# A hybrid decoder step: sample attention as one step generator, state update first in a chunk, values' split queued later

## The chip, the cores and the metric

One core of a Trainium2 chip. The metric is the device time of one launch in microseconds (us). The kernel is one program on the core's five engines: TensorE (PE in the profile) multiplies into PSUM, VectorE (DVE), ScalarE (ACT) and GpSimd (POOL) work element by element, SyncE (SP) issues nearly all DMAs. Each engine takes its instructions in the order in which they were written for it; they wait for one another by semaphores.

## What is computed

One step of a single decoder layer with two groups of heads. 512 prompt tokens and 8 x 8 sample tokens are normalised and projected together (576 columns); the result feeds sparse attention (8 heads, with an indexer that keeps 256 keys) and gated linear attention (GLA, 4 heads); both are gated and projected out.

```python
def dsa_sample(qa, ka, va, qi, ki, wi, cache_k, cache_v, cache_idx_k, page_table):
    ...
    sc = jnp.where(causal[None], index_scores(qi, wi, ki_all), -jnp.inf)
    _, idx = lax.top_k(sc, topk)
    ...
    return sparse_attend(qa, k_sel, v_sel, valid)

def gla(q, k, v, log_a, s0):
    def step(S, inp):
        ...
        o = o_inter + jnp.einsum('bhts,bhsv->bhtv', att, vt)
        S_new = jnp.exp(last)[:, :, 0, :, None] * S + jnp.einsum('bhsk,bhsv->bhkv', kt * jnp.exp(last - cum), vt)
        return S_new, o
```

The sample tokens' keys and values lie in pages of 128 tokens in device memory, found by a page table: 8 sequences of 8 pages.

## The kernel before, in words

All projections run in fp32 split into a high part and a remainder: a weight piece `w_raw` (256 KB) is loaded by SyncE (L178), cast to `w_hi` on ScalarE (L181), and the remainder `w_lo` is taken on VectorE (L183); three matmuls stand for one. `wload` holds this, `gemm` a projection of 128 outputs (ps_g, L219), `vgroup` one of 512 value columns, with the tokens as rows (L604 to L610).

**The sample units.** Sample attention is four `unit`s: two halves of the heads (`hg`) times two groups of four sequences (`w`). A unit reads its K pages in two halves of 16 pages (tile `kt`, four pages of 256 KB in a tile; matmuls `pS`), adds the new tokens, takes the softmax (`pr`, exponential at L780), transposes the probabilities (`pt`, L787, copied to `prT`), and reads its V pages in two halves (tile `vt`, matmuls `pOs`). I call the units 1 to 4 in their order, and a half of K or V a group; there are 16 groups. A unit is a Python generator with a `yield` behind each part; `fill()` (behind each half `gemm` and each second piece of `vgroup`) runs it on by a rate of 0.42 or 0.40 steps a fill. So the rate spreads the units between the projections. Tiles `kt` and `vt` share a pool of five buffers (units 1, 2) or four (3, 4). The page requests (`page_dma`) are written where the tile is used, and ordered on SyncE by `issue_after(paged[-3])`.

**The values.** `vgroup` copies its four token tiles out of PSUM as `v_tok` on ScalarE (L637), from where SyncE stores them to `sv` in device memory (L639); the samples' values go as `v_smp`. The tiles have tag `e1`, two buffers.

**GLA.** For each of four heads: `log_decay` (`ps_z`, from the loaded gate weights `wg`), `exps` (decay tiles `lv_d`, multiplied by k and q on VectorE, L994, L995), `decays` (transposed keys `kDt`, intra-chunk products `pl`), then `recur`. That one loads the head's values (`vtok`, and `vSg` for the samples), splits `vSg` into `vs` (four casts on ScalarE, L1069), and runs four chunks: output `pO`, state update `pUg`, copy `osb`, squares `jk` for the norm (L1086). Then come the samples: states `st` loaded for even and odd sequences, products into one `pO`, and updates `pUg` by `Kb` and `vs`. `ps_z`, `pO`, `pUg`, `pt`, `pl` and `ps_v` share three PSUM buffers (`pm`).

The heads' GLA is woven into the projections, so units 3 and 4, the value groups 2 and 3 and the GLA heads 0 to 3 run between 640 and 960 us. The order on each engine follows from the order of the text, from `high_priority(offset=WOFF)` (weights, and the matmuls of a `run` behind its first), from `issue_after`, and from when buffers come free; a scheduler settles it at build time.

```python
        with tc.issue_after(wloads[-1]):
            sy.dma_start(vtok, sv[:TP].rearrange("(i p) c -> p i c", p=P))
            sy.dma_start(vS[:TS], sv[TP:])
...
            with tc.issue_after(mark):
                for r0 in (0, 32):
                    se.copy(vs[w][r0 : r0 + 32], vS[r])
```

`mark` is the copy of `kDt` (L967).

Of the kernel before, what the change touches and what calls it, by code (L numbers as in the profile page):

```python
# [10 lines left out]
F32 = mybir.dt.float32  # L11
# [9 lines left out]
P = 128  # L21
# [98 lines left out]
def build(tc, I, O):  # L120
# [4 lines left out]
    R0, R1, RF = 0.42, 0.4, 1.1  # L125
# [21 lines left out]
    paged, wloads = [], []  # L147
# [447 lines left out]
    def vgroup(g, step):  # L595
# [39 lines left out]
        for i in range(4):  # L635
            vt = ev.tile([P, 512], F32, name="v_tok", tag="e1", bufs=2)
# [104 lines left out]
    def unit(un, w, hg, pages):  # L741
        span = 4
        qz = ev.tile([P, 4, 4, 32], F32, name="qz", tag="e0", bufs=2)
        po_.memset(qz, 0.0)
        for g in range(4):
            src = qaS[:, 4 * hg + g, 32 * w : 32 * w + 32].rearrange("p (b t) -> p b t", t=DT)
            dst = qz[:, g].rearrange("p b t -> p (b t)")
            dst = bass.AP(tensor=dst.tensor, offset=dst.offset, ap=[dst.ap[0], [40, 4], [1, DT]])
            po_.tensor_copy(dst, src)
        pr = un.tile([P, PAST + TS], F32, name="pr")  # L750
        mx = un.tile([P, 8], F32, name="mxs", bufs=2)
        lsel = [selw[:, 256 * half + P * w : 256 * half + P * (w + 1)] for half in range(2)]
        for half in range(2):
            S = pm.tile([P, 512], F32, name="pS", tag="pu", bufs=1)
            pe.matmul(S, lsel[half], biasS[:, :512], start=True, stop=False)
            for b0 in range(0, 4, span):
                mms = []
                for bb in range(b0, b0 + span):
                    kt = un.tile([P, 4, 512], F32, name="kt", tag="kv", bufs=pages)
                    page_dma(lambda j: kt[:, j, :], lambda r: I["ck"][r, hg].rearrange("o d c -> (o d) c"), (4 * w + bb) * NPAGE + 4 * half, 4)  # L760
                    kv = kt.rearrange("p j (g s) -> p j g s", g=4)
                    mms[:0] = [
                        partial(pe.matmul, S[32 * g : 32 * g + 32], qz[:, g, bb, :], kv[:, :, g, :], start=False, stop=(bb == 4 - span), tile_position=(0, 32 * g))
                        for g in range(4)
                    ]
                run(*mms)
                yield
            se.copy(pr[:, 512 * half : 512 * half + 512], S)
            ve.reduce_max(out=mx[:, half : half + 1], in_=pr[:, 512 * half : 512 * half + 512], axis=AX.X)
        S = pm.tile([P, 512], F32, name="pS", tag="pu", bufs=1)  # L770
        pe.matmul(S[:, :TS], lsel[1], biasS[:, 512:], start=True, stop=False)
        run(*(
            partial(pe.matmul, S[32 * g : 32 * g + 32, :TS], qaS[:, 4 * hg + g, 32 * w : 32 * w + 32], kaS[:, 4 * hg + g, :], start=False, stop=True, tile_position=(0, 32 * g))
            for g in range(4)
        ))
        se.copy(pr[:, PAST:], S[:, :TS])
        ve.reduce_max(out=mx[:, 2:3], in_=pr[:, PAST:], axis=AX.X)
        ve.reduce_max(out=mx[:, 3:4], in_=mx[:, 0:3], axis=AX.X)
        ve.tensor_scalar(out=mx[:, 3:4], in0=mx[:, 3:4], scalar1=-SCALE, scalar2=None, op0=ALU.mult)
        se.activation(pr, pr, AF.Exp, bias=mx[:, 3:4], scale=SCALE, accum_out=mx[:, 4:5])  # L780
        ve.reciprocal(out=mx[:, 7:8], in_=mx[:, 4:5])
        prT = un.tile([P, 9, P], F32, name="prT")
        for c in range(3):
            pt = mm1("pt")
            if c < 2:
                for j in range(4):
                    pe.transpose(pt[:, P * j : P * (j + 1)], pr[:, 512 * c + P * j : 512 * c + P * (j + 1)], ident)  # L787
                se.copy(prT[:, 4 * c : 4 * c + 4, :], pt.rearrange("p (j r) -> p j r", j=4))
            else:
                pe.transpose(pt[:, :P], pr[:, PAST + TS - P :], ident)  # L790
                se.copy(prT[:, 8, :], pt[:, :P])
        yield
        pO = pm.tile([P, 512], F32, name="pOs", tag="pu", bufs=1)
        for j0 in range(0, NPAGE, span):
            mms = []
            for j in range(j0, j0 + span):
                vt = un.tile([P, 4, 512], F32, name="vt", tag="kv", bufs=pages)
                page_dma(
                    lambda bb: vt[:, bb, :], lambda r: I["cv"][r, :, 512 * hg : 512 * hg + 512].rearrange("o s c -> (o s) c"),
                    NB * NPAGE + 4 * (NPAGE * w + j), 4,  # L800
                )
                mms[:0] = [
                    partial(
                        pe.matmul, pO[32 * g : 32 * g + 32].rearrange("p (b d) -> p b d", b=4), prT[:, j, 32 * g : 32 * g + 32],
                        vt[:, :, P * g : P * (g + 1)], start=(j == span - 1), stop=False, tile_position=(0, 32 * g),
                    )
                    for g in range(4)
                ]
            if j0 == NPAGE - span:
                mms += [  # L810
                    partial(
                        pe.matmul, pO[32 * g : 32 * g + 32].rearrange("p (b d) -> p b d", b=4), prT[:, 8, 32 * g : 32 * g + 32],
                        vaS[:, P * h : P * (h + 1)].unsqueeze(1).to_broadcast([P, 4, P]), start=False, stop=True, tile_position=(0, 32 * g),
                    )
                    for g in range(4) for h in (4 * hg + g,)
                ]
            run(*mms)
            yield
        ob = pr[:, :512]
        se.activation(ob, pO, AF.Copy, scale=mx[:, 7:8])  # L820
        pt = mm1("pt")
        for bb in range(4):
            pe.transpose(pt[:, P * bb : P * (bb + 1)], ob[:, P * bb : P * (bb + 1)], ident)
        src = bass.AP(tensor=pt.tensor, offset=pt.offset, ap=[pt.ap[0], [32, 4], [P + DT, 4], [1, DT]])
        sl = (slice(None), slice(4 * hg, 4 * hg + 4), slice(32 * w, 32 * w + 32))
        ve.tensor_tensor(
            out=mixS[sl].rearrange("p g (b t) -> p g b t", t=DT), in0=src,
            in1=gaS[sl].rearrange("p g (b t) -> p g b t", t=DT), op=ALU.mult,
        )
        yield  # L830
# [19 lines left out]
    us = chain(unit(un, 0, 0, 5), unit(un, 1, 0, 5))  # L850
    filler[:] = [us, R0, 0.0]
# [10 lines left out]
    us = chain(unit(un, 0, 1, 4), unit(un, 1, 1, 4))  # L862
    filler[:] = [us, R1, 0.0]
# [90 lines left out]
    def decays(h, qT, kT, cum, eL, kD, wide):  # L954
# [7 lines left out]
        def rows_of_k():  # L962
# [4 lines left out]
            mark = se.copy(kDt, pt.rearrange("p (i d) -> p i d", i=4))  # L967
# [5 lines left out]
            kept[h] = eL, qE, kDt, ks, getattr(mark, "ins", mark)  # L973
# [84 lines left out]
    def recur(h, eL, qE, kDt, ks, mark):  # L1058
# [17 lines left out]
        for i in range(4):  # L1076
            tsl = slice(P * i, P * (i + 1))
            pO = mm1("pO")
            pe.matmul(pO[:, :DV], att[:, i, :], vtok[:, i, :], start=True, stop=(S is None))
            pU = mm1("pUg")  # L1080
            pe.matmul(pU[:, :DV], kDt[:, i, :], vtok[:, i, :], start=True, stop=True)
# [4 lines left out]
            se.activation(jk, pO[:, :DV], AF.Square, accum_out=ss[:, i : i + 1])  # L1086
# [9 lines left out]
        pe.matmul(pO[:, :DV], attS, vS, start=True, stop=False)  # L1096
        for e in range(2):
            st = gl.tile([P, 4, DV], F32, name="st", bufs=2)
            sview = lambda x: x[h].rearrange("p (m e) v -> p m e v", e=2)[:, :, e, :]
            sy.dma_start(st, sview(I["state"]))  # L1100
            for m in range(4):
                mp_ = slice(32 * m, 32 * m + 32)
                pe.matmul(pO[mp_, :DV], Qb[:, 2 * m + e, :], st[:, m, :], start=False, stop=(e == 1), tile_position=(0, 32 * m))
# [254 lines left out]
```

## Time and profile before

| | |
|---|---|
| median of 3 runs | 1238.5 us (1237.82 to 1240.36) |
| profiled execution | 1241.06 us, its span 1239.3 us |
| TensorE busy | 1216.5 us (98%) |
| VectorE, ScalarE, GpSimd busy | 662.8, 564.6, 301.8 us |
| mean granted clock of TensorE | 0.995 |
| moved | 209.42 MB, 169 GB/s over the span |

The profile's page gives busy times, a strip of 40 slices, the DMA queues, the chain of waits and the costliest groups of instructions. An engine's idle time matters only where TensorE, the busiest, waits for it. The granted clock is given in parts of 2.4 GHz; a mean between 0.5 and 1 over a stretch means that a part of it ran at 1.2 GHz.

### The profile page before, as it was taken

What the parts mean: (1) busy time and instruction counts of PE and PEld (TensorE: products, weight loads), DVE (VectorE), ACT (ScalarE), POOL (GpSimd) and SP (SyncE); (2) the same over time, 40 slices, a digit from 0 to 9 for tenths busy, and PEclk for the clock granted to TensorE, in tenths of its full rate; (3) what the DMA queues carried; (4) which work ended last, traced back from release to release, by engine and by line L of the source; (5) the groups of instructions that cost most, each with busy time, mean ns of one, the idle gap of its engine ahead of it and who ended that gap; (6) DMA issues with size and microseconds to landing.
All of it is one profiled execution on the core that took longest, in us unless ns stands there. A gap on an engine that the chain in (4) does not pass through costs nothing.

```text
span 1239.3 us, 23602 instructions
## 1 busy us (share of the span) xinstructions
PE 1216.5 (98%) x8699; PEld 1073.9 (87%) x8699; DVE 662.8 (53%) x1326; ACT 564.6 (46%) x1079; POOL 301.8 (24%) x471
## 2 busy tenths in 40 slices
PE   9999999999999999999999989999999999999996
PEld 8899987899997878898987778678999998888896
DVE  6679899699744314434545244425566463223233
ACT  7967655453443323443444253435566462223233
POOL 1224567445411201010105210301124020202021
PEclk9999999999999999999999999999999999999999
DMA  9642233423457596753667573765525364333335
GB/s 315 219 151 91 65 108 101 158 86 104 162 176 243 181 314 207 254 190 139 218 206 248 188 261 111 267 214 199 168 75 186 106 204 145 107 96 121 94 107 174
DMA packets 126885, 209.42 MB, mean 169 GB/s; under 512 B 14497, under 2 KB 37554, under 8 KB 126066
## 3 DMA queue, kind: packets, MB, share of 16 engines
q1 hardware_dynamic: 125682, 206.47, 50.7%
q8 instruction: 68, 1.11, 0.4%
q10 hardware_dynamic: 1088, 1.45, 0.4%
q14 instruction: 47, 0.39, 0.1%
HBM read 184.52 MB, written 23.22 MB: 168 GB/s over the span
## 4 chain that ended last, share of the span: by engine, by line
PE 86%; DVE 5%; DMA 4%; ACT 2%; issue 1%; SPq 1%; POOL 0%; ACTq 0%; DVEq 0%; POOLq 0%
PE ps_g L219 36%; PE ps_g L227 6%; PE acc L1224 5%; PE acc L1223 5%; PE acc L1222 5%; PE ps_g L608 4%; PE ps_g L610 4%; PE ps_g L609 4%; PE pOs L255 2%; PE pS L255 2%; PE acc L1227 1%; PE acc L1226 1%; DMA vSg<-sv 1%; PE ps_v L604 1%; PE ps_v L605 1%
## 5 line engine op out<-in xcount | busy, mean ns | idle before, releaser
L181 ACT CAST w_hi<-w_raw 128x512 fp32r<-128x512 f32 x316 | 193.4, 619 | 371.7 <-PE ps_g L219 135.0
L183 DVE TENSOR_TENSOR w_lo<-w_raw,w_hi 128x512 fp32r<-128x512 f32 x252 | 177.8, 712 | 308.2 <-ACT w_hi L181 286.8
L219 PE MATMUL ps_g<-xh,w_hi 128*128 128x288 f32 x1312 | 289.0, 299 | 1.4 <-issue 1.0
L219 PE MATMUL ps_g<-xl,w_hi 128*128 128x288 f32 x1312 | 287.9, 298 | 0.0
L219 PE MATMUL ps_g<-xh,w_lo 128*128 128x288 f32 x1312 | 286.4, 297 | 0.0
L219 PEld LDWEIGHTS ps_g<-xh,w_hi 128*128 128x128 f32 x1312 | 213.6, 189 | 10.0 <-issue 5.8
L219 PEld LDWEIGHTS ps_g<-xl,w_hi 128*128 128x128 f32 x1312 | 213.1, 189 | 2.0 <-issue 1.2
L219 PEld LDWEIGHTS ps_g<-xh,w_lo 128*128 128x128 f32 x1312 | 213.4, 189 | 1.2 <-DVE w_lo L199 0.2
L1223 PE MATMUL acc<-w_lo,mh 128*128 128x512 f32 (+1 forms) x320 | 110.7, 346 | 0.0
L1224 PE MATMUL acc<-w_hi,ml 128*128 128x512 f32 (+1 forms) x320 | 110.7, 346 | 0.0
L1222 PE MATMUL acc<-w_hi,mh 128*128 128x512 f32 (+1 forms) x320 | 110.3, 346 | 0.0
L608 PE MATMUL ps_g<-w_hi,xh 128*128 128x512 f32 x256 | 101.5, 398 | 0.0
L610 PE MATMUL ps_g<-w_hi,xl 128*128 128x512 f32 x256 | 100.1, 391 | 0.0
L609 PE MATMUL ps_g<-w_lo,xh 128*128 128x512 f32 x256 | 99.8, 390 | 0.0
L183 POOL TENSOR_TENSOR w_lo<-w_raw,w_hi 128x512 fp32r<-128x512 f32 x64 | 86.4, 1353 | 51.8 <-ACT w_hi L181 38.7
L1242 POOL TENSOR_TENSOR y<-y,nfb 128x512 f32<-128x512 f32 (+3 forms) x25 | 27.7, 1121 | 186.8 <-ACT yjk L1241 186.8
L1223 PEld LDWEIGHTS acc<-w_lo,mh 128*128 128x128 f32 x320 | 60.5, 189 | 7.5
L1222 PEld LDWEIGHTS acc<-w_hi,mh 128*128 128x128 f32 x320 | 60.4, 189 | 7.5
L1224 PEld LDWEIGHTS acc<-w_hi,ml 128*128 128x128 f32 x320 | 60.4, 189 | 7.5
L608 PEld LDWEIGHTS ps_g<-w_hi,xh 128*128 128x128 f32 x256 | 48.0, 188 | 13.1 <-issue 2.5
L610 PEld LDWEIGHTS ps_g<-w_hi,xl 128*128 128x128 f32 x256 | 48.1, 188 | 11.2 <-issue 0.8
L609 PEld LDWEIGHTS ps_g<-w_lo,xh 128*128 128x128 f32 x256 | 48.1, 188 | 9.5
(339 smaller groups left out, 1952.8 us busy)
## 6 DMA issues: line engine op xcount, KB each, us to landing
w_raw<-in_w SPq DMA_DIRECT2D x188, 256.0 KB, 3.0
kt<-in_ck SPq DMA_DIRECT2D x128, 256.0 KB, 5.1
vt<-in_cv SPq DMA_DIRECT2D x128, 256.0 KB, 5.4
w_raw<-in_wv SPq DMA_DIRECT2D x64, 256.0 KB, 3.0
w_raw<-in_wo SPq DMA_DIRECT2D x64, 256.0 KB, 2.7
xr<-in_xT SPq DMA_DIRECT2D x16, 288.0 KB, 4.6
xt<-in_xp SPq DMA_DIRECT2D x4, 1024.0 KB, 7.5
sv<-v_tok SPq DMA_DIRECT2D x16, 256.0 KB, 3.3
```

What stands on the lines that cost most here:

```text
L181: se.copy(hi, raw)
L183: lo_eng[0].tensor_tensor(out=lo, in0=raw, in1=hi.bitcast(F32), op=ALU.subtract)
L219: pe.matmul(ps[:, j, :HT], wt, xt[:, j * HT : (j + 1) * HT], start=(k == 0 and n == 0), stop=(k == NK - 1 and n == 2),)
L227: pe.matmul(ps[:, 0, :TQ], wt[:, c], xt[:, P:T], start=(k == 0 and n == 0), stop=(k == NK - 1 and n == 2))
L255: f()
L608: pe.matmul(accs[i], xh[k][:, c], wh, start=a, stop=False)
L609: pe.matmul(accs[i], xh[k][:, c], wl, start=False, stop=False)
L610: pe.matmul(accs[i], xl[k][:, c], wh, start=False, stop=b)
L1222: pe.matmul(acc, mh[k][:, tsl], wh, start=(k == 0), stop=False)
L1223: pe.matmul(acc, mh[k][:, tsl], wl, start=False, stop=False)
L1224: pe.matmul(acc, ml[k][:, tsl], wh, start=False, stop=(k == NK - 1))
L1242: po_.tensor_tensor(out=yc, in0=yc, in1=nfb[:r, cs], op=ALU.mult)
```

## The change

Five parts, all in the order and the buffers; the arithmetic stays.

- `unit` becomes one generator `units` for both units of a half of the heads. It takes exactly one step a fill (rate 1.0): `rest(n)` pads it with empty steps. `fetch` asks for the next group's 16 pages right behind the step that used the group before.
- `v_tok` takes turns between tags `e1` and `e0`, two buffers each (`e0` is also that of `qz`, `oT` and others).
- In `recur`, `vSg` is loaded ahead of `vtok`, and the casts `vs` are issued behind the last `w_hi` cast written so far (`rounded[-1]`), not behind the copy of `kDt`.
- In a chunk the state update `pUg` goes ahead of the output `pO`; `jk` squares `osb` (SBUF), not `pO` (PSUM).
- Both state tiles are loaded first; the eight products with `st` come in one run, then the updates.

```diff
-    R0, R1, RF = 0.42, 0.4, 1.1
+    RF = 1.1
...
-            se.copy(hi, raw)
+            c = se.copy(hi, raw)
+            rounded.append(getattr(c, "ins", c))
...
-            vt = ev.tile([P, 512], F32, name="v_tok", tag="e1", bufs=2)
+            vt = ev.tile([P, 512], F32, name="v_tok", tag=("e1", "e0")[i % 2], bufs=2)
...
-    def unit(un, w, hg, pages):
+    def units(un, hg, pages):
+        def fetch(w, part, half):
+            out = []
+            for n in range(4 * half, 4 * half + 4):
+                t = un.tile([P, 4, 512], F32, name=("kt", "vt")[part], tag="kv", bufs=pages)
+                if part:
+                    page_dma(
...
+                out.append(t)
+            return out
+        def rest(n):
+            for _ in range(n):
+                yield
+        kv = fetch(0, 0, 0)
+        yield
+        for w in range(2):
...
+            for half in range(2):
...
+                run(*mms)
+                yield
+                kv = fetch(w, half, 1 - half)
+                se.copy(pr[:, 512 * half : 512 * half + 512], S)
+                ve.reduce_max(out=mx[:, half : half + 1], in_=pr[:, 512 * half : 512 * half + 512], axis=AX.X)
+                if not half:
+                    yield from rest(3)
...
+            se.activation(pr, pr, AF.Exp, bias=mx[:, 3:4], scale=SCALE, accum_out=mx[:, 4:5])
+            ve.reciprocal(out=mx[:, 7:8], in_=mx[:, 4:5])
+            yield
...
+            yield from rest(2)
+            pO = pm.tile([P, 512], F32, name="pOs", tag="pu", bufs=1)
+            for half in range(2):
...
+                run(*mms)
+                yield
+                if not half:
+                    kv = fetch(w, 1, 1)
+                    yield from rest(3)
+                elif w == 0:
+                    kv = fetch(1, 0, 0)
...
+            yield from rest(2)
...
-    us = chain(unit(un, 0, 1, 4), unit(un, 1, 1, 4))
-    filler[:] = [us, R1, 0.0]
+    us = units(un, 1, 4)
+    filler[:] = [us, 1.0, 0.0]
...
         with tc.issue_after(wloads[-1]):
+            sy.dma_start(vS[:TS], sv[TP:])
             sy.dma_start(vtok, sv[:TP].rearrange("(i p) c -> p i c", p=P))
-            sy.dma_start(vS[:TS], sv[TP:])
...
-            with tc.issue_after(mark):
+            with tc.issue_after(rounded[-1]):
...
+            pU = mm1("pUg")
+            pe.matmul(pU[:, :DV], kDt[:, i, :], vtok[:, i, :], start=True, stop=True)
             pO = mm1("pO")
             pe.matmul(pO[:, :DV], att[:, i, :], vtok[:, i, :], start=True, stop=(S is None))
-            pU = mm1("pUg")
-            pe.matmul(pU[:, :DV], kDt[:, i, :], vtok[:, i, :], start=True, stop=True)
...
-            se.activation(jk, pO[:, :DV], AF.Square, accum_out=ss[:, i : i + 1])
+            se.activation(jk, osb[:, i, :], AF.Square, accum_out=ss[:, i : i + 1])
...
+        sts = [gl.tile([P, 4, DV], F32, name="st", bufs=2) for _ in range(2)]
         for e in range(2):
-            st = gl.tile([P, 4, DV], F32, name="st", bufs=2)
-            sy.dma_start(st, sview(I["state"]))
-            for m in range(4):
-                pe.matmul(pO[mp_, :DV], Qb[:, 2 * m + e, :], st[:, m, :], start=False, stop=(e == 1), tile_position=(0, 32 * m))
+            sy.dma_start(sts[e], sview(I["state"], e))
+        run(*(
+            partial(pe.matmul, pO[32 * m : 32 * m + 32, :DV], Qb[:, 2 * m + e, :], sts[e][:, m, :], start=False, stop=(e == 0), tile_position=(0, 32 * m))
+            for e in (1, 0) for m in range(4)
+        ))
```

Three places show how the instructions move. Line numbers behind the change are some 27 higher in this part of the program (L1069 becomes L1096, L780 becomes L806).

SyncE between value group 2 and the values' load of head 0, before. `w_raw` are weight pieces, `kt` pages of K for unit 4, `sv` the stores of the values; `TENSOR_LOAD` and `ISA` read page numbers.

```order
L178 DMA w_raw<-in_w 128x512 x2
L639 DMA sv_475<-v_tok 128x512 x3
L178 DMA w_raw<-in_w 128x512
L639 DMA sv_475<-v_tok 128x512
L178 DMA w_raw<-in_w 128x512
L152 TENSOR_LOAD ptab
```

The same place of SyncE with the change:

```order
L178 DMA w_raw<-in_w 128x512 x2
L640 DMA sv_475<-v_tok 128x512 x4
L152 TENSOR_LOAD ptab
L157 ISA
L157 DMA kt<-in_ck 128x512
L157 ISA
L157 DMA kt<-in_ck 128x512
L178 DMA w_raw<-in_w 128x512 x2
L1090 DMA vtok<-sv_475 128x4x256
```

The four stores stand together, and two K pages stand ahead of the two weight pieces that stood between and behind the stores. Further on, `vSg` still follows `vtok`, two pages, the store of `v_smp` and eight more pages.

ScalarE at the softmax of unit 4 and the split of head 1's sample values (`vs`), before.

```order
L181 CAST w_hi<-w_raw 128x512 x3
L1069 CAST vs_10335<-vSg 32x256 x2
L181 CAST w_hi<-w_raw 128x512
L1069 CAST vs_10336<-vSg 32x256 x2
L776 COPY pr<-pS 128x64
L780 ACTIVATE pr,mxs<-pr,mxs 128x1088
L637 ACTIVATE v_tok<-ps_g,sst 128x512 x2
```

The same place of ScalarE with the change:

```order
L802 COPY pr<-pS 128x64
L806 ACTIVATE pr,mxs<-pr,mxs 128x1088
L181 CAST w_hi<-w_raw 128x512 x2
L815 COPY prT<-pt 128x512 x2
L638 ACTIVATE v_tok<-ps_g,sst 128x512 x2
L818 COPY prT<-pt 128x128
L638 ACTIVATE v_tok<-ps_g,sst 128x512 x2
L181 CAST w_hi<-w_raw 128x512
L1096 CAST vs_10391<-vSg 32x256 x2
L1096 CAST vs_10392<-vSg 32x256 x2
```

The score copy and the exponential stood behind the four casts `vs`; now the casts stand behind them, and behind the copies of the transposed probabilities and the four `v_tok`.

TensorE at the first chunks of head 0, before; `ps_g` is a projection that fills the gaps.

```order
L219 MATMUL ps_g<-xl,w_hi 128x288 x2
L1079 MATMUL pO<-vtok,att 128x256
L1081 MATMUL pUg<-vtok,kDt 128x256
L1079 MATMUL pO<-vtok,att 128x256
L219 MATMUL ps_g<-xh,w_hi 128x288 x2
```

The same place of TensorE with the change:

```order
L220 MATMUL ps_g<-xl,w_hi 128x288 x2
L1106 MATMUL pUg<-vtok,kDt 128x256
L1108 MATMUL pO<-vtok,att 128x256
L1106 MATMUL pUg<-vtok,kDt 128x256
L220 MATMUL ps_g<-xh,w_hi 128x288 x2
```

The three PSUM buffers go to an output, an update and an output before, and to an update, an output and an update now; the output of the second chunk comes after the gap.

## Rows read from the trace of the kernel before

**Rows 1.** The page: span, and TensorE in part 1 (busy us, share, instructions).
```profile
span 1239.3 us, 23602 instructions
...
PE 1216.5 (98%) x8699; PEld 1073.9 (87%) x8699; DVE 662.8 (53%) x1326; ACT 564.6 (46%) x1079; POOL 301.8 (24%) x471
```

**Rows 2.** Waits of TensorE: who waited for whom, us in total, times, longest.
```profile
PE pt L787 <- ACT pr L780: 2.9, 1, 2.9
PE pUg L1081 <- ACT jk L1086: 2.1, 1, 2.1
PE pOs L252 <- DMA vt<-in_cv: 1.8, 1, 1.8
...
PE ps_g L219 <- issue: 1.0, 1, 1.0
PE pl L252 <- DVE lv_d L995: 1.0, 1, 1.0
```

**Rows 3.** Stretches: length, busy us of five engines, clock, DMA share, GB/s.
```profile
720.00:740.00 20.00, 17.94 (x124) 17.13 (x123) 9.58 (x17) 12.42 (x24) 5.25 (x8) 0.97 0.94 325
740.00:760.00 20.00, 20.00 (x128) 17.88 (x127) 10.46 (x27) 6.66 (x18) 0.24 (x1) 0.94 0.25 78
...
820.00:840.00 20.00, 17.15 (x119) 13.64 (x118) 7.02 (x15) 12.62 (x24) 0.00 (x0) 0.91 0.50 154
...
960.00:1220.00 260.00, 260.00 (x1521) 232.29 (x1520) 97.12 (x171) 86.71 (x185) 31.32 (x26) 1.00 0.40 123
```

**Rows 4.** Timeline, SyncE, unit 3 and head 0: start, length, line, what, count.
```profile
696.76 11.45 SPq L157 DMA_DIRECT2D vt<-in_cv  x16
...
709.25 7.84 SPq L639 DMA_DIRECT2D sv<-v_tok  x3
...
718.42 0.38 SPq L639 DMA_DIRECT2D sv<-v_tok  x1
...
721.87 0.38 SPq L1062 DMA_DIRECT2D vtok<-sv  x1
722.30 0.52 SPq L647 DMA_DIRECT2D sv<-v_smp  x1
723.02 5.91 SPq L157 DMA_DIRECT2D kt<-in_ck  x8
729.05 0.48 SPq L1063 DMA_DIRECT2D vSg<-sv  x1
```

**Rows 5.** Timeline, ScalarE, head 0; in brackets the idle time before, and its releaser.
```profile
734.47 1.66 ACT L1069 CAST vs<-vSg 32x256 fp32r<-32x256 f32 x4 [2.75 <-DMA vSg<-sv]
...
736.68 0.36 ACT L1084 COPY osb<-pO 128x256 f32<-128x256 f32 x1
736.95 0.39 ACT L1086 ACTIVATE jk<-pO 128x256 f32<-128x256 f32 x1
```

**Rows 6.** Timeline, ScalarE, unit 4 and head 1.
```profile
820.09 0.84 ACT L1069 CAST vs<-vSg 32x256 fp32r<-32x256 f32 x2 [7.63 <-DMA vSg<-sv]
...
822.44 0.21 ACT L776 COPY pr<-pS 128x64 f32<-128x64 f32 x1
```

**Rows 7.** Timeline, TensorE, V projection ahead of V's second half.
```profile
710.29 0.39 PE L608 MATMUL ps_g<-w_hi,xh 128*128 128x512 f32 x1
710.52 0.39 PE L609 MATMUL ps_g<-w_lo,xh 128*128 128x512 f32 x1
```

**Rows 8.** Timeline, TensorE: the first eight transposes of units 3 and 4.
```profile
689.75 1.03 PE L787 MATMUL pt<-c_ident,pr 128*128 128x128 f32 x8
...
824.94 1.97 PE L787 MATMUL pt<-c_ident,pr 128*128 128x128 f32 x8 [2.85 <-ACT pr L780]
```

**Rows 9.** Timeline, VectorE, head 3.
```profile
952.29 0.74 DVE L911 TENSOR_TENSOR og<-ps_g,rstd 128x576 f32<-128x576 f32 x1
```

**Rows 10.** Timeline, head 0: `ps_z` on TensorE, last early decay product on VectorE.
```profile
643.47 0.42 PE L896 MATMUL ps_z<-abS,wgS 128*128 128x288 f32 x2
...
659.37 0.45 DVE L995 TENSOR_TENSOR lv_d<-lv_d,qT 128x256 f32<-128x256 f32 x1
```

More of the change, by code (lines that the diff above doesn't have):

```diff
@@ L145, in cload @@
         return t
[L147 removed]
+    paged, wloads, rounded = [], [], []
     def page_dma(dst, src, ix, n):
@@ L757, in unit @@
                 mms = []
[L758 to L761, printed above, removed]
+                for bb in range(4):
+                    k4 = kv[bb].rearrange("p j (g s) -> p j g s", g=4)
                     mms[:0] = [
-                        partial(pe.matmul, S[32 * g : 32 * g + 32], qz[:, g, bb, :], kv[:, :, g, :], start=False, stop=(bb == 4 - span), tile_position=(0, 32 * g))
+                        partial(pe.matmul, S[32 * g : 32 * g + 32], qz[:, g, bb, :], k4[:, :, g, :], start=False, stop=(bb == 0), tile_position=(0, 32 * g))
@@ L767, in unit @@
                 yield
[L768 to L783, printed above, removed]
-            pt = mm1("pt")
[L785 to L829, printed above, removed]
@@ L830, in unit @@
-        yield
+                kv = fetch(w, half, 1 - half)
[3 more added lines that the diff above has]
+                    yield from rest(3)
+            S = pm.tile([P, 512], F32, name="pS", tag="pu", bufs=1)
+            pe.matmul(S[:, :TS], lsel[1], biasS[:, 512:], start=True, stop=False)
+            run(*(
+                partial(pe.matmul, S[32 * g : 32 * g + 32, :TS], qaS[:, 4 * hg + g, 32 * w : 32 * w + 32], kaS[:, 4 * hg + g, :], start=False, stop=True, tile_position=(0, 32 * g))
+                for g in range(4)
+            ))
@@ new lines, in units @@
+            se.copy(pr[:, PAST:], S[:, :TS])
+            ve.reduce_max(out=mx[:, 2:3], in_=pr[:, PAST:], axis=AX.X)
+            ve.reduce_max(out=mx[:, 3:4], in_=mx[:, 0:3], axis=AX.X)
+            ve.tensor_scalar(out=mx[:, 3:4], in0=mx[:, 3:4], scalar1=-SCALE, scalar2=None, op0=ALU.mult)
+            se.activation(pr, pr, AF.Exp, bias=mx[:, 3:4], scale=SCALE, accum_out=mx[:, 4:5])
+            ve.reciprocal(out=mx[:, 7:8], in_=mx[:, 4:5])
+            yield
+            prT = un.tile([P, 9, P], F32, name="prT")
@@ new lines, in units @@
+            for c in range(3):
+                pt = mm1("pt")
+                if c < 2:
+                    for j in range(4):
+                        pe.transpose(pt[:, P * j : P * (j + 1)], pr[:, 512 * c + P * j : 512 * c + P * (j + 1)], ident)
+                    se.copy(prT[:, 4 * c : 4 * c + 4, :], pt.rearrange("p (j r) -> p j r", j=4))
+                else:
+                    pe.transpose(pt[:, :P], pr[:, PAST + TS - P :], ident)
+                    se.copy(prT[:, 8, :], pt[:, :P])
@@ new lines, in units @@
+            yield from rest(2)
+            pO = pm.tile([P, 512], F32, name="pOs", tag="pu", bufs=1)
+            for half in range(2):
+                mms = []
+                for j in range(4):
+                    mms[:0] = [
+                        partial(
+                            pe.matmul, pO[32 * g : 32 * g + 32].rearrange("p (b d) -> p b d", b=4), prT[:, 4 * half + j, 32 * g : 32 * g + 32],
+                            kv[j][:, :, P * g : P * (g + 1)], start=(not half and j == 3), stop=False, tile_position=(0, 32 * g),
+                        )
+                        for g in range(4)
+                    ]
+                if half:
+                    mms += [
+                        partial(
+                            pe.matmul, pO[32 * g : 32 * g + 32].rearrange("p (b d) -> p b d", b=4), prT[:, 8, 32 * g : 32 * g + 32],
+                            vaS[:, P * h : P * (h + 1)].unsqueeze(1).to_broadcast([P, 4, P]), start=False, stop=True, tile_position=(0, 32 * g),
+                        )
+                        for g in range(4) for h in (4 * hg + g,)
+                    ]
+                run(*mms)
[5 more added lines that the diff above has]
+                    kv = fetch(1, 0, 0)
@@ L849, in build @@
     un, un_s = pool("unit", 1, side="right")
-    us = chain(unit(un, 0, 0, 5), unit(un, 1, 0, 5))
-    filler[:] = [us, R0, 0.0]
+    us = units(un, 0, 5)
+    filler[:] = [us, 1.0, 0.0]
     for h in range(4, HA):
@@ L966, in rows_of_k @@
             kDt = gl.tile([P, 4, P], F32, name="kDt")
-            mark = se.copy(kDt, pt.rearrange("p (i d) -> p i d", i=4))
+            se.copy(kDt, pt.rearrange("p (i d) -> p i d", i=4))
             pt = mm1("pt")
```

59 lines of the change are left out of this document (39 added, 20 removed).

## Prediction

> **What bounds the kernel now.** I read the page first: span and busy time of each engine. TensorE is busy for 1216.5 of 1239.3 us [rows 1], so no faster helper can give more than the 22.8 us in which it stands still, unless it also lifts a lowered clock. Second came TensorE's waits, which say where it stands still and for whom [rows 2]: in the stage of sample pages and gated linear attention there are 2.9 us for the exponential of a unit, 2.1 us for the square `jk`, 1.8 us for pages of V, 1.0 us for a decay tile, 1.0 us that the profile gives to nobody ("issue"): 8.8 us. The rest lies at the two ends of the program and in small waits ahead of this stage, where the diff changes little.
>
> Third came the stretches, for the clock [rows 3]. It is granted in full (2.4 GHz) in the long tail, but at 0.97 and 0.94 in the 40 us around the wait for `jk`, and at 0.91 in the 20 us around the wait for the exponential; after those waits TensorE runs at the lower level (1.2 GHz) for a moment. 20 us x (0.03 + 0.06) = 1.8 us, and 20 us x 0.09 = 1.8 us at most. So a wait of some 2 us costs nearly twice its length, and what this stage can give back is at most 8.8 + 3.6 = 12.4 us.
>
> Fourth came the timelines of SyncE and ScalarE, for the causes. V's pages: sixteen requests go out one behind the other from 696.76 for 11.45 us, with no other work between [rows 4]. `jk`: SyncE stands for 7.84 us in the three stores of `v_tok`; the load of `vtok`, the store of `v_smp`, eight K pages and last the load of `vSg` follow, the latter at 729.05 [rows 4]. ScalarE waits 2.75 us for that load at the first copy `vs`, and the queue behind it (a cast, then `osb` at 736.68 and `jk` at 736.95) is late by as much [rows 5]; TensorE needs the PSUM buffer that `jk` reads last. The exponential: ScalarE stands 7.63 us at `vs` for the next head's `vSg`, and the score copy `pr`, ahead of the exponential, is queued behind it [rows 6].
>
> **The change, part by part.** No matmul is added or removed, and no byte: it moves work and changes buffers. So the sum is one of waits.
>
> *V's second half, unit 3.* Its pages can only be asked for when the first half has freed the buffers. Counted in the two orders of TensorE, 42 matmuls `ps_g` of 128x512 stand between the two halves before and 48 after; all others there are the same. Consecutive matmuls of that kind start 0.23 us apart [rows 7], so the second half comes 6 x 0.23 = 1.4 us later against its pages. The wait of 1.8 falls to 0.4: **-1.4 us**. Ends: 0, if the requests slip by the same time, and -1.8.
>
> *`jk`, head 0.* `v_tok` gets four buffers for two, so ScalarE no longer waits for two stores to land, and SyncE's three stores need not take 7.84 us; the single store and loads around them take 0.38 us [rows 4], so SyncE could be 7.84 - 3 x 0.38 = 6.7 us earlier. The K pages also need the buffers that V's second half gives back; this half comes earlier by the 1.4 us above and no more. The load of `vSg` must come 2.75 us earlier to take away ScalarE's wait [rows 5], and 1.4 us more because TensorE itself arrives earlier: 4.2 of the 6.7 that are there. I take it as gone: 2.1 of waiting and 1.8 of clock, **-3.9 us**. Without it the reordered chunk still helps a little: `jk` reads SBUF, so the PSUM buffer is free when `osb` is copied and not when `jk` has read it, 0.3 us later [rows 5]. Ends: -0.3 and -3.9. That `jk` now reads SBUF, and that the update goes ahead of the output, costs TensorE nothing: the same matmuls, side by side.
>
> What the row shows of `vSg` here: issued at 729.05 behind the pages, in a stretch where the DMA engines moved 325 GB/s [rows 3], and read at 734.47, 5.4 us later. The Trainium skill ("DMA: Bandwidth & Descriptors", section on queues, rings and completion order) says that each DMA engine takes the descriptors of one queue in the order in which they were put there. By that rule loading `vSg` ahead of `vtok` gains nothing at this head, since the new order has it behind the pages all the same, and only the shorter stop of SyncE counts; it is the first rival below.
>
> *The exponential, unit 4.* The new order of ScalarE has score copy and exponential ahead of all four `vs`, behind which they stood. The wait of 2.9 us goes. So does most of the clock's loss: eight transposes took 1.97 us here and 1.03 us in the unit before [rows 8], 0.9 us, and the stretch bounds the loss by 1.8; part of the lowered clock lies in the wait itself, so I take 1.4, between the two. Sum **-4.3 us**; ends -1.0, if ScalarE stands for something else there, and -4.7. Who is late next: the `vs` copies, now behind `v_tok`. They feed the sample states' updates, which TensorE reaches after the prompt's chunks.
>
> *The decay tile, head 3.* On VectorE `og` (0.74 us) stood directly ahead of the last two products of `lv_d` [rows 9]; now it stands behind them. Of the wait of 1.0 it takes **-0.7 us**. The "issue" of 1.0 us behind it I leave. Ends: 0 and -2.0.
>
> *Both state loads ahead, eight matmuls in one run.* Two loads for one at a time: the pool has two buffers already, and none of TensorE's waits names them [rows 2]. Nothing either way.
>
> *What it may add.* The units' steps are set anew at all 32 fills. The first head's `ps_z` stands behind the load `wg`, and that now behind some fifteen K-page requests, where it had been ahead of them; counted by its matmuls, `ps_z` moves 13 us later. It ran at 643.47, and the last decay product that does not need the transposes ended at 659.82 [rows 10]: a chain of 16.4 us. The first user of those products, `pl`, is by the new order 21.8 us of matmuls behind `ps_z`, which leaves 5.4 us. The nearest rows for a chain that comes late all the same are the waits themselves, from 1.0 to 2.9 us and with clock 3.9. Ends: nothing, and +3.9; I take the smallest, **+1.0 us**.
>
> Sum: -1.4 - 3.9 - 4.3 - 0.7 + 1.0 = -9.3 us. The profiled execution took 1241.06 us; this would be 1231.8 there. It lies 2.6 us over the median of 1238.5 (and 0.7 over the highest of the three), and its waits are the program's order, not that run's chance, so I carry the difference over to the median: **1229.2 us**.
>
> **Rivals.** *The pages still bound `vSg`.* The transfers in front of it are the same, and if K's buffers come free late, the load goes out late whatever SyncE does. For it: the 325 GB/s, the order; against it: 6.7 us at hand for 4.2. Then `jk`'s wait stays: -9.3 + 3.9 = -5.4, 1233.1 us. Chance 0.20.
>
> *The waits move.* `wg` sits behind a stop of SyncE like the 7.84 us, which eats the 5.4 us and leaves 2.4 of waiting, 4.2 with the clock, on top of the first rival: -9.3 + 3.9 + 4.2 = -1.2, 1237.3 us, within 0.2% (2.5 us, about what a measurement of this kernel can tell from no change). Against it: the stop of 7.84 has its cause in `v_tok`, and that is taken away. Chance 0.12.
>
> *Slower: weights behind pages.* One queue, SyncE's, carries weight pieces and pages in order. Where a page's request waits for its buffer, the pieces wait too. A piece in the V projection feeds 14 matmuls, 14 x 0.23 = 3.2 us [rows 7], with five buffers for the cast pieces. A run of sixteen pages, 11.45 us, did not make TensorE wait for weights [rows 2, 4]. A stop like the 7.84 us inside such a run makes 19.3 us, 7.8 more than what is known to be covered; twice that, against a gain of 9.3, gives +6.3, 1244.8 us. It decides from about 5.9 us at each of two such places. For it: requests are now made at once when the step that used the buffers is written down, so they can stand further ahead in the queue. Against it: in the new order the runs are no longer than they were, sixteen at most, with pieces before and after. Chance 0.08.
>
> **How the numbers follow.** Forecast 0.60, rivals 0.20, 0.12 and 0.08. The forecast's own range goes from all that the stage can give, 1238.5 - 12.4 = 1226.1, to the first rival. The range takes in that rival and the second: 1226.0 to 1237.5 us, leaving out the slower case and a little on either side. Faster by over 0.2% means under 1236.0: the forecast and the first rival, 0.79 after a small deduction; within: 0.12; slower: 0.09.
>
> **What would show it.** In the profile after, TensorE's waits should no longer name the exponential and `jk`; V's pages should stand there with under 1 us. Windows of 20 us in the stage should grant 0.99 or 1.00 throughout. SyncE should pass the four `v_tok` stores in under 3 us, and ScalarE should have no wait at `vs` over 3 us with an exponential behind it. TensorE's busy time should fall by some 3 us, by the clock alone, and its idle time by some 6. The forecast is wrong if a wait of over 2 us appears at `ps_z`, at `pl`, at the first K group of unit 3, or on weights.

## The result and the profile after

| | before | changed |
|---|---|---|
| median | 1238.92 us (1237.82 to 1240.36, 4 runs) | 1231.33 us (1230.14 to 1232.90, 4 runs) |
| ratio, 95% interval | | 0.9939 (0.9922 to 0.9956) |
| profiled execution | 1241.06 us, span 1239.3 | 1232.90 us, span 1231.1 |

The kernel became faster by 7.6 us, 0.6%, with an interval from 0.44 to 0.78%. Forecast were 9.3 us, from 1238.5 to 1229.2.

The page of the changed kernel, part 1 (busy us, share of the span, instructions):

```profile
PE 1214.7 (99%) x8693; PEld 1073.2 (87%) x8699; DVE 660.1 (54%) x1326; ACT 564.8 (46%) x1077; POOL 297.9 (24%) x471
```

TensorE's busy time fell by 1.8 us (some 3 were forecast) and its idle time from 22.8 to 16.4, 6.4 us (some 6 were forecast) [rows 1]. The waits of TensorE (who waited for whom; us in total, times, longest):

```profile
PE ps_g L228 <- ACT w_hi L181: 1.4, 1, 1.4
...
PE pl L253 <- ACT w_hi L181: 0.7, 1, 0.7
```

The exponential, `jk` and V's pages [rows 2] are gone from the list; of the stage a wait at `pl` stands, 0.7 us for the 1.0 of the decay tile (the profile names a cast here; in e9, below, it names the decay tile, with 0.9 us). Five waits of 0.16 us ("issue") stand ahead of K groups, one of them in the stage. The first row lies in the first 340 us. The stretches (length, busy us of five engines, clock, DMA share, GB/s), first one of the program's head and then those of [rows 3]:

```profile
40.00:60.00 20.00, 18.30 (x83) 15.99 (x82) 10.79 (x19) 19.39 (x31) 3.93 (x5) 0.91 0.62 207
...
720.00:740.00 20.00, 20.00 (x142) 19.58 (x141) 9.53 (x16) 11.81 (x26) 5.24 (x8) 1.00 0.82 284
740.00:760.00 20.00, 20.00 (x129) 17.32 (x129) 11.14 (x29) 5.94 (x14) 0.24 (x1) 1.00 0.36 113
820.00:840.00 20.00, 20.00 (x152) 17.21 (x149) 11.86 (x20) 14.17 (x27) 5.51 (x8) 1.00 0.89 313
```

The clock is now granted in full in all three stretches of the stage, which had 0.97, 0.94 and 0.91. The head lost time: in the same 40 to 60 us the kernel before had

```profile
40.00:60.00 20.00, 18.83 (x94) 16.73 (x93) 10.28 (x20) 19.09 (x31) 3.28 (x5) 1.00 0.63 201
```

Up to there the order of every engine is the same in both kernels, so this difference (0.5 us more idle and 20 x 0.09 = 1.8 us of clock) is one of executions and not of the change.

ScalarE at the exponential of unit 4, in the timeline of the changed kernel:

```profile
804.67 0.21 ACT L802 COPY pr<-pS 128x64 f32<-128x64 f32 x1
806.07 1.20 ACT L806 ACTIVATE pr<-pr,mxs 128x1088 f32<-128x1088 f32 x1 [1.18 <-DVE mxs L805]
...
820.60 1.66 ACT L1096 CAST vs<-vSg 32x256 fp32r<-32x256 f32 x4
```

Score copy and exponential run at 804.67 and 806.07, and the four `vs` at 820.60 have no idle time ahead of them where they had 7.63 us [rows 6].

At head 0 the second profiled execution of the changed kernel (experiment e9, whose head kept the full clock) compares best with the one before. SyncE's timeline:

```profile
708.27 3.62 SPq L640 DMA_DIRECT2D sv<-v_tok  x4
...
724.59 0.48 SPq L1089 DMA_DIRECT2D vSg<-sv  x1
```

The four stores take 3.62 us without a stop where three took 7.84 (under 3 were forecast), and `vSg` goes out at 724.59 for 729.05 [rows 4]. ScalarE's, VectorE's and TensorE's:

```profile
728.90 1.67 ACT L1096 CAST vs<-vSg 32x256 fp32r<-32x256 f32 x4 [2.34 <-DMA vSg<-sv]
```

```profile
731.72 0.41 DVE L1116 COPY Sst<-pUg 128x256 f32<-128x256 f32 x1
```

```profile
732.47 0.59 PE L1108 MATMUL pO<-vtok,att 128*128 128x256 f32 x2
```

ScalarE still waits at `vs`, 2.34 us for 2.75 [rows 5], since it gets there sooner as well. But VectorE's copy `Sst`, which now frees the buffer of the second output, ends at 732.13, and TensorE comes to that output at 732.47.

### The profile page after: what moved, and what is told of

Read it like the earlier page. It is cut to its first block, busy times and chain, and to the rows that moved or that the text cites. A ratio compares the mean times of both kernels' runs of the same rounds, so it can differ in the third digit from the quotient of the medians.

```text
span 1231.1 us, 23603 instructions
## 1 busy us (share of the span) xinstructions
PE 1214.7 (99%) x8693; PEld 1073.2 (87%) x8699; DVE 660.1 (54%) x1326; ACT 564.8 (46%) x1077; POOL 297.9 (24%) x471
## 4 chain that ended last, share of the span: by engine, by line
PE 90%; DVE 4%; DMA 3%; ACT 1%; issue 1%; SPq 0%; POOL 0%; DVEq 0%; ACTq 0%; POOLq 0%
PE ps_g L220 37%; PE ps_g L609 5%; PE acc L1253 5%; PE acc L1254 5%; PE acc L1252 5%; PE ps_g L611 5%; PE ps_g L610 5%; PE ps_g L228 4%; PE pOs L256 2%; PE pS L256 2%; DMA xt<-in_xp 1%; PE ps_v L605 1%; PE acc L1257 1%; PE acc L1256 1%; DMA xr<-in_xT 1%; PE ps_v L606 1%
```

## Experiments: one part alone

The first four kernels are the one before with one part of the change each. Their 21 executions of the kernel before had a median of 1238.51 us.

**e1: `v_tok` on four buffers.**

```diff
-            vt = ev.tile([P, 512], F32, name="v_tok", tag="e1", bufs=2)
+            vt = ev.tile([P, 512], F32, name="v_tok", tag=("e1", "e0")[i % 2], bufs=2)
```

> The kernel before, with v_tok alone on four buffers. My theory (two buffers made ScalarE and then SyncE stop, so vSg went out late and jk was late): SyncE's stores of value group 2 take under 3 us instead of 7.84, TensorE's wait for jk is gone (2.1 us and 1.8 of clock), the waits for the exponential (2.9) and for V's pages (1.8) stay: about 1235 us, 3.9 under before. Rival (the pages ahead of vSg set its time, whatever SyncE does): jk's wait stays over 1.5 us, 1238 to 1239 us.

Measured: 1233.76 us, ratio 0.9964 (0.9950 to 0.9978), 4.7 us less. SyncE's timeline and TensorE's waits:

```profile
708.30 3.56 SPq L639 DMA_DIRECT2D sv<-v_tok  x4
...
723.91 0.48 SPq L1063 DMA_DIRECT2D vSg<-sv  x1
```

```profile
PE pt L787 <- ACT pr L780: 1.8, 1, 1.8
...
PE pOs L252 <- DMA vt<-in_cv: 0.3, 1, 0.3
```

`vSg` goes out 5.1 us earlier, and no wait for `jk` is left. The rival falls: it was not the pages ahead of `vSg` that set its time. The stores take 3.56 us and not under 3. The wait for V's pages was expected to stay, and is 0.3 us here with the old order; more on that below.

**e2: the generator.** The diff is the function `units` as printed ahead, with its two uses and the rate 1.0.

> The kernel before, with the step generator alone. My theory: V's pages wait under 1 us (six more matmuls between the halves, -1.4), the exponential stands ahead of the vs copies by the new order and its wait is gone (-4.3), jk's wait stays since v_tok still has two buffers: about 1233.2 us. Rival (the generator does it all, the other parts nothing): no wait over 1 us left, 1231 to 1232 us.

Measured: 1239.53 us, ratio 1.0010 (0.9997 to 1.0023): no change. Both theories fail. TensorE's waits, and ScalarE at unit 4:

```profile
PE pUg L1107 <- ACT jk L1112: 3.3, 2, 2.1
PE ps_z L922 <- ACT prT L817: 1.6, 1, 1.6
```

```profile
804.47 1.21 ACT L805 ACTIVATE pr<-pr,mxs 128x1088 f32<-128x1088 f32 x1 [1.19 <-DVE mxs L804]
...
813.91 1.67 ACT L1095 CAST vs<-vSg 32x256 fp32r<-32x256 f32 x4 [5.85 <-DMA vSg<-sv]
...
822.57 0.69 ACT L637 ACTIVATE v_tok<-ps_g,sst 128x512 f32<-128x512 f32 x1 [4.21 <-DMA sv<-v_tok]
823.16 0.26 ACT L817 COPY prT<-pt 128x128 f32<-128x128 f32 x1
```

The exponential (804.47) is out in time, as the order showed. But the `vs` copies still go to ScalarE behind the copy of `kDt`, so that they come next, wait 5.85 us for `vSg`, and hold the copies `prT`; then the third `v_tok` waits 4.21 us for a buffer with the last `prT` behind it (823.16), and TensorE waits for that at `ps_z`, 1.6 us. `jk` waits twice, 3.3 us in all. The stand was moved along the queue, not removed.

**e3: the split later.**

```diff
+            sy.dma_start(vS[:TS], sv[TP:])
             sy.dma_start(vtok, sv[:TP].rearrange("(i p) c -> p i c", p=P))
-            sy.dma_start(vS[:TS], sv[TP:])
...
-            with tc.issue_after(mark):
+            with tc.issue_after(rounded[-1]):
```

> The kernel before, with vSg loaded ahead of vtok and the vs copies behind the last w_hi cast. My theory: the exponential is ahead of the vs copies, its wait (2.9 us and 1.4 of clock) is gone; V's pages (1.8) and jk (2.1 and 1.8 of clock) stay: about 1234.6 us. Rival (the load order alone brings vSg early enough at head 0 too): jk's wait gone as well, 1230.7 us. Rival (vs later on ScalarE makes the sample updates late): a new wait of TensorE for vs or Kb, 1237 us or more.

Measured: 1234.38 us, ratio 0.9970 (0.9955 to 0.9985), 4.1 us less. TensorE's waits:

```profile
PE pUg L1082 <- ACT jk L1087: 1.7, 1, 1.7
...
PE pOs L253 <- DMA vt<-in_cv: 0.7, 1, 0.7
```

As my theory had it: the exponential's wait is gone with no generator, `jk`'s stays (1.7 for 2.1), no new one came. Both rivals fall.

**e4: update first.**

```diff
+            pU = mm1("pUg")
+            pe.matmul(pU[:, :DV], kDt[:, i, :], vtok[:, i, :], start=True, stop=True)
             pO = mm1("pO")
             pe.matmul(pO[:, :DV], att[:, i, :], vtok[:, i, :], start=True, stop=(S is None))
-            pU = mm1("pUg")
-            pe.matmul(pU[:, :DV], kDt[:, i, :], vtok[:, i, :], start=True, stop=True)
...
-            se.activation(jk, pO[:, :DV], AF.Square, accum_out=ss[:, i : i + 1])
+            se.activation(jk, osb[:, i, :], AF.Square, accum_out=ss[:, i : i + 1])
```

> The kernel before, with the state update first in a chunk and jk read from osb. My theory: the PSUM buffer comes free 0.3 us sooner, ScalarE is still held by vSg: jk's place in the waits goes to osb with about 1.8 us, 1238.6 us, no change that can be told. Rival (the order of the PSUM buffers is what made TensorE wait, since the update of the second chunk now has its buffer before the gap): that wait is gone with its clock, about 1235 us.

Measured: 1245.14 us, ratio 1.0051 (1.0035 to 1.0067): 6.6 us slower. Neither theory had that. TensorE's waits:

```profile
PE pl L252 <- DVE lv_d L995: 3.5, 1, 3.5
PE pO L1081 <- DVE Sst L1089: 2.1, 1, 2.1
PE pt L787 <- ACT pr L780: 1.6, 1, 1.6
PE pOs L252 <- DMA vt<-in_cv: 1.4, 1, 1.4
```

At head 0 the wait has a new name and its old length: the second output now takes the buffer of the first update, which VectorE frees with its copy `Sst`, and VectorE stands at the remainder of `vs`. The longest wait is at head 3's decay tiles, which the edit doesn't touch. GpSimd's timeline there:

```profile
944.02 1.53 POOL L915 TENSOR_TENSOR og<-og,mo 128x576 f32<-128x576 f32 x1 [4.39 <-ACT w_hi L181]
945.51 1.11 POOL L935 TENSOR_TENSOR lv_d<-cum 128x288 f32<-128x288 f32 x1
```

The product of the first gate (`og` times `mo`, 944.02) stands in GpSimd's queue ahead of the last two pairs of decay differences, where in the kernel before only the very last of them stands behind it. It idles 4.39 us, which the profile puts down to a cast; the load `mo` had gone out at 938.39, and the longest landing of `mo` in this trace is 5.5 us. TensorE waits 3.5 us for those decay tiles.

The waits do not make up the loss, since others are shorter here than in the kernel before. From its profiled execution to this one the span grew by 4.0 us; TensorE's idle time fell by 0.5 us, and its busy time rose by 4.5:

```profile
PE 1221.0 (98%) x8699; PEld 1075.5 (87%) x8699; DVE 661.2 (53%) x1326; ACT 565.3 (45%) x1077; POOL 300.3 (24%) x471
```

The clock does not explain it: the stretches below 1.00 (two of 0.91 here, printed further down; 0.97, 0.94 and 0.91 before [rows 3]) cost either execution 20 us x 0.18 = 3.6 us. One piece can be named. Before, the sixteen products of a head with the state tiles `st` stand together:

```profile
748.45 1.07 PE L1103 MATMUL pO<-st,Qb 128*32 128x256 f32 x16
```

Here an update breaks them in two:

```profile
744.20 1.05 PE L1103 MATMUL pO<-st,Qb 128*32 128x256 f32 x10
745.18 0.38 PE L1109 MATMUL pUg<-vs,Kb 96*128 96x256 f32 x1
745.49 0.63 PE L1103 MATMUL pO<-st,Qb 128*32 128x256 f32 x6
```

Over the four heads these products take 6.3 us for 4.3. The rest of the 4.5 us is not settled.

## Experiments: one part undone

The next four are the changed kernel with one part taken back; the kernel before, beside them, had a median of 1237.78 us (22 executions).

**e5: `v_tok` on two buffers again** (the diff of e1, reversed).

> The changed kernel, with v_tok on two buffers again. My theory, after the four parts alone: the buffers cured the late vSg of head 0, and no other part replaces them. SyncE stops 6 to 8 us in the stores again, vSg goes out 4 to 5 us later, and TensorE waits 1 to 2.1 us for jk or Sst at head 0: 1233 to 1235.5 us. Rival (with the generator's longer distances vSg comes early enough all the same): no wait over 0.5 us there, 1231.4 us as the changed kernel.

Measured: 1234.58 us, ratio 0.9969 (0.9960 to 0.9979). TensorE's wait, and SyncE:

```profile
PE pO L1108 <- DVE Sst L1116: 2.3, 1, 2.3
```

```profile
708.64 5.89 SPq L640 DMA_DIRECT2D sv<-v_tok  x3
...
726.55 0.48 SPq L1089 DMA_DIRECT2D vSg<-sv  x1
```

SyncE stops for 5.89 us (expected 6 to 8), `vSg` goes out 2.0 us later than in e9 (expected 4 to 5), and TensorE waits 2.3 us at head 0 (expected 1 to 2.1). The buffers are needed, as in e1, and no other part takes their place.

**e6: the old units and rates** (the diff of e2, reversed).

> The changed kernel with the old units and their rates of 0.42 and 0.40. My theory: the generator alone brought nothing (1239.5 beside 1238.5) since it moved the stand of ScalarE from the exponential to the copies prT; with the split queued later this is cured already, so what is left of it is V's pages, 0.3 to 1.8 us in the executions seen: 1231.5 to 1233.5 us. Rival (the generator's order is what keeps the reordered chunk from the 3.5 us of wait at the decay tile of head 3 that the chunk alone showed): a wait over 2 us at pl, 1234.5 us or more.

Measured: 1231.14 us, ratio 0.9951 (0.9936 to 0.9966). The waits of the stage:

```profile
PE pl L253 <- ACT w_hi L181: 0.8, 1, 0.8
PE pOs L253 <- DMA vt<-in_cv: 0.6, 1, 0.6
```

Without the generator all is as with it, but for 0.6 us at V's pages. The theory holds, with a time 0.4 us under its range, and the wait at `pl`, which the rival had over 2 us, is 0.8.

**e7: `vtok` first and the split behind `kDt` again** (the diff of e3, reversed).

> The changed kernel with vtok loaded ahead of vSg and the vs copies behind the copy of kDt. My theory: as in the generator alone, the exponential is out, but vs stands on ScalarE ahead of the copies prT of unit 4; vSg comes earlier than there because v_tok has four buffers, so the wait of 1.6 at ps_z shrinks but stays, and jk of head 1 waits too: 1232.5 to 1235 us. Rival (by order of the exponential alone): nothing comes back, 1231.4 us.

Measured: 1235.03 us, ratio 0.9978 (0.9968 to 0.9988): the size that I expected, at another place. There is no wait at `ps_z` or `jk`; there is one at head 3, and GpSimd's timeline shows the same picture as in e4:

```profile
PE pl L253 <- DVE lv_d L1022: 3.5, 1, 3.5
```

```profile
935.12 1.42 POOL L942 TENSOR_TENSOR og<-og,mo 128x576 f32<-128x576 f32 x1 [5.11 <-DMA w_raw<-in_w]
```

GpSimd idles 5.11 us ahead of the gate's product, with two pairs of decay differences behind it. The profile puts that down to a weight load; the product's own load `mo` had gone out at 930.62, and its landings take up to 4.7 us in this trace. The changed kernel has the same order on GpSimd, but there the product waits 1.73 us:

```profile
933.62 1.43 POOL L942 TENSOR_TENSOR og<-og,mo 128x576 f32<-128x576 f32 x1 [1.73 <-DMA mo<-so]
```

So the order alone does not make the wait; it also takes a late load. Why SyncE sent that load later here than in the changed kernel I did not settle.

**e8: output first and `jk` from PSUM again** (the diff of e4, reversed).

> The changed kernel with the output ahead of the update in a chunk and jk read from pO. Alone this part cost 6.6 us, by the order that it gave GpSimd and VectorE at head 3. My theory: its direct effect is nothing, and in the changed kernel the wait at head 3 is only 0.7, so undoing it changes little: 1231 to 1232 us. Rival (it costs here as well): 1227 to 1229 us. Rival (it is needed with the rest, as the PSUM order suggests): a wait for jk returns, 1233 us or more.

Measured: 1230.15 us, ratio 0.9937 (0.9924 to 0.9951), beside 0.9939 of the changed kernel. The waits of the stage:

```profile
PE ps_g L220 <- issue: 1.3, 1, 1.3
...
PE pl L253 <- DVE lv_d L1022: 0.5, 1, 0.5
```

No wait for `jk` returned, and the time lies 0.9 us under my range and 1.2 over that of the first rival. Within the changed kernel this part does nothing that these runs can tell.

## Experiments: what suffices

The kernel before, beside these, had a median of 1237.49 us (11 executions).

**e9: the changed kernel again**, with no edit.

> The changed kernel once more, beside the others of this call. Both theories: 1230.5 to 1232 us, ratio 0.992 to 0.996.

Measured: 1230.15 us, ratio 0.9938 (0.9918 to 0.9957), just under the range. Its rows stand above.

**e10: the buffers and the later split, nothing else** (the diffs of e1 and e3 on the kernel before).

> The kernel before with two of the five parts: v_tok on four buffers, and vSg ahead of vtok with the vs copies behind the last w_hi cast. My theory: these two hold all of the gain, 4.7 + 4.1 us as each showed alone: 1229 to 1231 us, as good as all five parts; waits of TensorE in the stage: pages of V 0.3 to 1, the decay tile of head 3 up to 1.3, none for jk or the exponential. Rival (the generator and the reordered chunk carry a share): 1233 us or more.

Measured: 1230.93 us, ratio 0.9943 (0.9922 to 0.9965). The waits of the stage:

```profile
PE pOs L253 <- DMA vt<-in_cv: 0.8, 1, 0.8
PE ps_g L220 <- issue: 0.7, 1, 0.7
PE pl L256 <- issue: 0.7, 1, 0.7
```

Two parts of five give what all five give, as far as these runs tell. The fifth part (the state tiles loaded first, their products in one run) was not tried by itself; e10 does without it. The parts alone sum up: 4.7 + 4.1 = 8.8 us, beside 1237.49 - 1230.93 = 6.6 here.

**e11.** Its label names an edit that was not made: as the expectation says, the kernel is that of e4.

> Placeholder of the update-first part alone, seen once more: with the gates' products on GpSimd in their old place; 1243 to 1246 us, and the wait of 3.5 us at pl with GpSimd at the gate product before it.

Measured, in a single execution: 1247.22 us (1.2 over the range), with 3.6 us of wait at `pl`, and again GpSimd at the gate's product:

```profile
945.47 1.87 POOL L915 TENSOR_TENSOR og<-og,mo 128x576 f32<-128x576 f32 x1 [4.64 <-DMA mo<-so]
```

It confirms e4, the 6.3 us of state products and the raised busy time (1222.7 us) too, and adds that GpSimd's idle time here is put down to the load `mo` by name. Update first with the product written later was not tried.

**e12: the two parts, and the gates' products behind head 3's recurrence.**

```diff
-    def gate(i):
+    def gate(i, late=None):
...
-        o_t = ev.tile([P, T], F32, name="mo", tag="e0", bufs=2)
-        sy.dma_start(o_t, spill_o[i])
-        (po_ if i < 7 else ve).tensor_tensor(out=g1, in0=g1, in1=o_t, op=ALU.mult)
         og.append(g1)
+        def finish():
+            o_t = ev.tile([P, T], F32, name="mo", tag="e0", bufs=2)
+            sy.dma_start(o_t, spill_o[i])
+            (po_ if i < 7 else ve).tensor_tensor(out=g1, in0=g1, in1=o_t, op=ALU.mult)
+        finish() if late is None else late.append(finish)
...
+            lates = []
             for i in range(3):
-                gate(i)
+                gate(i, lates)
...
         recur(h, *kept[h])
+        if h == 3:
+            for f in lates:
+                f()
```

> The two parts of e10, with the products of the first three gates (og times mo, on GpSimd) written behind head 3's recurrence, so that no decay tile stands behind a wait for mo. My theory: the wait at pl falls under 0.4 us, 0.5 to 1.3 us less than e10: 1228.5 to 1230 us, faster than the changed kernel. Rival (VectorE's chain sets that wait, not GpSimd's): no difference from e10.

Measured: 1229.64 us, ratio 0.9935 (0.9915 to 0.9954). This is the longest wait that is left in the stage, and there is none at head 3:

```profile
PE pOs L253 <- DMA vt<-in_cv: 0.5, 1, 0.5
```

The wait at `pl` and the "issue" behind it are gone, with the product out of the queue. The time is the lowest of e9 to e12 by 0.5 us, less than the intervals can tell: it is the cleanest trace, but not shown to beat the changed kernel.

## Why the prediction was right, and where not

**The bound.** TensorE's waits in the stage and the clock after them were read as all that can be had, 12.4 us, and the gain came from there: the three larger waits are gone and the clock is full. From the profiled execution before to that after the time fell by 8.2 us; with the 0.6 + 0.5 us of idle time and the 1.8 us of clock that the latter lost in its first 60 us, some 11 us were gained behind them.

**The sum.** Its waits without the clock give 1.4 + 2.1 + 2.9 + 0.7 - 1.0 = 6.1 us, with the clock 9.3; measured were 7.6 and, in e9, 7.3. The term that was mis-sized is the clock, 1.8 + 1.4 us. It holds for the profiled execution before, in which TensorE went to 1.2 GHz behind both waits. I carried it over to the median as "the program's order, not that run's chance", and that is the step that failed: the same wait costs clock in one execution and not in another. In e4 TensorE waited 2.1 us at head 0 with the clock at 1.00 behind it, and 1.6 us at the exponential with 0.91:

```profile
720.00:740.00 20.00, 17.89 (x126) 17.27 (x124) 9.40 (x17) 12.27 (x25) 5.23 (x8) 1.00 0.91 309
740.00:760.00 20.00, 20.00 (x129) 17.19 (x128) 11.46 (x30) 6.33 (x15) 0.24 (x1) 1.00 0.36 113
...
820.00:840.00 20.00, 18.25 (x126) 14.52 (x125) 7.81 (x15) 13.45 (x23) 2.37 (x4) 0.91 0.57 185
...
940.00:960.00 20.00, 16.52 (x241) 16.10 (x241) 11.96 (x26) 9.30 (x18) 9.03 (x13) 0.91 0.41 133
```

In e2 it waited 2.1 us for `jk` of head 1, again at full clock:

```profile
840.00:860.00 20.00, 17.88 (x131) 16.32 (x130) 10.17 (x26) 8.69 (x23) 0.24 (x1) 1.00 0.34 113
```

That profiled execution of e2 took 1235.79 us, the least of the eleven, which went up to 1243.8. The executions of the kernel before spread over 1234.7 to 1243.7 us, those of the changed kernel over 1229.5 to 1232.9.

That spread goes with the clock. The record has a mean clock for every execution, to three places, the program's end included. Of the 54 executions of the kernel before beside e1 to e12, the five at 0.994 or 0.995 took 1241.2 us on average, the eleven at 0.996 took 1239.3, and the 38 at 0.997 or 0.998 took 1237.3. A difference of 0.003 in 1216.5 us of busy time is 3.6 us (an estimate); the means at the two ends lie 3.9 apart. The profiled execution from which the clock's 3.2 us were read had 0.995 and so was one of the slow few: most executions of the kernel before had little of that to give back. From 1237.3 to e9's 1230.15 it is 7.2 us, nearer to the 6.1 without the clock.

**`jk`, by the buffers: right.** e1 and e5 show it from both sides. The working was partly off: ScalarE's wait for `vSg` was to go, and 2.34 of 2.75 us stayed; enough that the chain ended 0.3 us ahead of TensorE. The rule of the Trainium skill ("DMA: Bandwidth & Descriptors", section on queues, rings and completion order), by which loading `vSg` ahead of `vtok` gains nothing at head 0, agrees with e3: `vSg` still went out there behind `vtok` and eight pages, and `jk` waited 1.7 us. No run has it ahead of the pages, so none tests the rule further.

**The exponential, by the order: right, but by the wrong part.** I let the new order of ScalarE speak for the whole change. The later split cures it alone (e3). The generator puts the exponential ahead as well, but alone it leaves `vs` in front of `prT`, and the wait comes back as `jk` and `ps_z` (e2).

**V's pages, by the generator: right in the traces, not to be seen in the times.** The wait went from 1.8 to nothing where 0.4 was expected. The six traces with the generator (the changed kernel, e2, e5, e7, e8, e9) have no such wait; the eight with the old units all have it, with 1.8, 0.3, 0.7, 1.4, 0.6, 0.8, 0.8 and 0.5 us in the kernel before, e1, e3, e4, e6, e10, e11 and e12. So the generator does take it away, but the wait varies with the execution, and 1.8 is its highest. In time the generator costs and gains nothing that can be told, alone (1.0010) or undone (0.9951 beside 0.9938).

**"Update first costs TensorE nothing": wrong alone, right within the change.** I counted its matmuls, and those are the same. What I didn't count is what comes to stand beside them: alone, the edit broke the runs of products with `st`, which made TensorE's busy time longer, and at head 3 it put a gate's product ahead of two pairs of decay differences in GpSimd's queue. In the changed kernel the runs are whole. The fifth part writes them as one run; that this is what keeps them whole was not tried.

**The decay tile.** 0.7 us forecast, 0.3 and 0.1 found (0.7 and 0.9 us of wait in the two profiled executions). `og` on VectorE was moved as said. I had not read GpSimd's queue, where the gate's product stands between the decays; with that out of it no wait is left (e12).

**The added cost.** 1.0 us was taken for chains that come late; the five small waits ahead of K groups make 0.8 us, and e9 has none over 0.15 there. No wait at `ps_z`, at the first K group of unit 3 or on weights appeared, so the second and third rival did not come to pass, nor the first.

## What to carry to other kernels

A wait of the busiest engine is cured at the instruction that stands in the queue, not at the one that is late: look for what an in-order engine has in front of it that waits for a DMA, and move that behind everything that is due sooner, or give it the buffers with which it needn't wait. Moving the late instruction ahead only hands the stand to the next one in the queue. Where a scheduler settles the order, try each part of a change alone: here two of five parts held the gain, one did nothing to the time, one cost half a per cent by itself, with a wait and with broken runs of products at places that its edit doesn't touch, and one was not tried alone. And before a lowered clock in one profiled execution goes into a forecast of the median, see how many executions have it.

## What was not expected of the hardware

The clock behind a wait: 1.6 us of waiting was followed by 0.91 in 20 us, 2.1 us by 1.00, and the 2.1 us of the kernel before by 0.97 and 0.94 [rows 3]. The length of a wait does not tell alone whether it costs clock.

Sixteen page requests, sent out in one unbroken run of 10.9 to 11.5 us in the kernel before, e1, e3 and e4, were waited for by TensorE for 1.8, 0.3, 0.7 and 1.4 us: how long this wait is in a single trace says little.
